# Four small steps after each 192-slot step, joint transposes and alternating block order in a mixture-of-experts stage on one Trainium2 core

## The chip, the cores and the metric

The kernel runs on one core of a Trainium2 chip. The metric is the device time of one execution in microseconds (us), the median of several runs. Engine names: PE is the matrix engine (PEld its weight loads), DVE the vector engine, ACT the scalar engine, POOL the general one, SP the engine whose queue issues the weight transfers.

## The reference, cut to what matters

The reference is a hybrid layer (state space and attention) followed by a second block of two layers, on 256 tokens of width 1024. The change lies wholly in the last stage, the mixture of experts of the second layer:

```
logits = x @ w_router                     # 256 tokens, 8 experts
top_vals, top_idx = top_k(logits, 2)      # two experts for each token
gates = softmax(top_vals)
y = (silu(xb @ w1[e]) * (xb @ w3[e])) @ w2[e]   # for each expert e, on its tokens xb
out = segment_sum(y * gate)               # 1024 -> 3584 -> 1024, in float32
```

After it come a residual sum and a layer norm. Every expert has 3 x 1024 x 3584 float32 weights, 44 MB, so the stage reads 352 MB.

## The kernel before, in words

The experts are ranked by load on the device and renamed: rank 0 has the fewest tokens and so on as the code fixes it. Each rank has a capacity in slots: rank 1 has 192 (a block of 128 slots and one of 64, the latter called number NE = 8), ranks 2 and 3 have 128, ranks 0, 4, 5, 6 and 7 have 64. A block's tokens are gathered into SBUF by one-hot matmuls (`gather`, L1399: matmuls L1416, evictions L1421 and L1423, transposed one-hots L1431, gates L1432).

**A step** is a pair (rank, j): one seventh (512 of 3584 columns) of one expert, NJ = 7 steps for each rank, 56 in all. The list `STEPS` (L218) gives their order. A step reads six weight units of 1 MB, each one transfer into one `raw` buffer: two of w1 and two of w3 (`hidden`, L1510) and two of w2 (`down`, L1571). The matmuls of `down` for step i-1 are placed behind those of `hidden` for step i (`passes`, L1443), and `_moe_order` (L206) gives the units in that order to `rows_unit`, which issues the transfers on SP's queue. From step 2 on six `raw` buffers are in rotation (1 of raw4, 2 of raw2, 3 of rawp; `narrow`, L1306, takes three out), so a transfer waits until the sixth unit before it has been used up.

**Two kinds of block.** A 64-slot block multiplies in plain float32, straight from `raw`, in column pairs (`pair`, L1568: even k into PSUM partitions 0 to 63, odd k into 64 to 127; the two halves are added after a transpose, `turned`, L1550). One such product of one unit shows as 8 PE instructions. A 128-slot block multiplies split operands (`mm3`, L317 to L319, 12 PE instructions a unit); for ranks 1, 2 and 3 (`WIDE`) every unit is therefore split first, in two halves, by a cast on ACT (L298) and a subtraction on DVE (L299).

**After the products of w1 (s) and w3 (t).** For a 64-slot block both are copied to SBUF tiles `eg` by ACT (L1527, three buffers). s is transposed inside `hidden`, behind the first unit of w3 (L1523); t is transposed in `later`, between the two halves of the previous step's `down`. Each transposed product takes a PSUM tile `tp` (two buffers), four PE instructions (L1554) and a reduction on DVE (L1558) that frees it; then silu (L1545) and the product with t (L1546). A 128-slot block multiplies s and t on DVE (L1536), transposes the result (L1539) in one `tp`, and splits it (ACT L354, DVE L355). The first transpose of each group is tied, in PE's order, to the PE instruction traced just before it (`keep_in_program_order`, L1541 and L1556). The rest of each engine's order is fixed by a scheduler when the program is built; on the chip each engine keeps that order.

**PSUM.** Three banks `acc`, three `sm`, two `tp`. A block that is not `aside` accumulates over its seven steps in two `sm` banks. A block that is `aside` (NE, 4, 5, 6 and 7) takes an `acc` and a `sm` bank for each step and adds them into an SBUF tile `y` (DVE L1588; ACT L1586 the first time). When a rank is through, its result is scaled and scattered into the residual (`scaled`, `scatter` L1610).

The order before, as ranks: 0 0 0 4 0 4 0 4 0 4 0 4 4 4, then seven times 1 5 6 7, then seven times 2, then seven times 3. The gathers come in five groups: {4}, {1, NE, 5}, {6, 7}, {2}, {3}; up to step 5 a group is gathered just before its first use, afterwards two steps ahead of it.

Of the kernel before, what the change touches and what calls it, by code (L numbers as in the profile page):

```python
# [8 lines left out]
F32 = mybir.dt.float32  # L9
# [8 lines left out]
P = 128  # L18
D = 1024
# [14 lines left out]
NE = 8  # L34
# [179 lines left out]
    return out  # L214

STEPS = _steps((0, 0, 0, 4, 0, 4, 0, 4, 0, 4, 0, 4, 4, 4) + (1, 5, 6, 7) * NJ + (2,) * NJ + (3,) * NJ)  # L218

WIDE = (1, 2, 3)  # L220

WHOLE = [a + i for a in (0, 52) for i in (1, 2, 3, 4, 15, 16)]

FIXED = [e for e, _ in _moe_order(STEPS)].index(4)

# [14 lines left out]
class Kern:  # L242
# [916 lines left out]
    def moe(self, l, h, hT, out):  # L1159
# [6 lines left out]
        with ExitStack() as ctx:  # L1166
# [142 lines left out]
            def widen():  # L1309
                rctx.close()  # L1310
                more = ctx.enter_context(tc.tile_pool(name="more", bufs=1, side="right"))
                self.xgs = [more] * 4
                self.xns = [more] * 3 + self.xns
                self.ohs = [more] * 4 + self.ohs
                self.ya = more
            es = [nc.sync.value_load(who[0:1, i:i + 1], min_val=0, max_val=NE - 1) for i in range(1, NE)]
# [5 lines left out]
            def rows():  # L1322

                for i in range(2):
                    t = self.ya.tile([P, D], F32, name=f"y{5 + i}")
                    for c in range(2):
                        acc = self.bank([P, 4, P], "acc")
                        for k in range(4):
                            at = KD * i + 4 * c + k
                            mm(acc[:, k], self.gb[:, at:at + 1].to_broadcast([P, P]), self.ident, start=True, stop=True)  # L1330
                        nc.scalar.copy(t[:, 512 * c:512 * c + 512], acc.rearrange("p a b -> p (a b)"))
                    gb.append(t)
                fin.extend(self.ya.tile([P, D], F32, name=n) for n in ("y7", "y8"))
                stats.append(self.mp.tile([P, NT, 2, 6], F32, name="stats"))

            def done(sums):
                self.last_norm(r, sums, fin, stats[0], *gb, out)
            self.passes(posp, gatep, STEPS, r, first, [
                {4: [(4, b)]}, {1: [(1, a), (NE, b)], 5: [(5, b)]},
                {6: [(6, b)], 7: [(7, b)]}, {2: [(2, a)]}, {3: [(3, a)]}], (NE, 4, 5, 6, 7), {2: narrow, 3: widen, len(STEPS) - NJ: rows}, done)  # L1340
            n = nc.values_load(who[0:1, NE + 4:], min_val=0, max_val=4)
            with ExitStack() as some:
                for i in range(4):
# [55 lines left out]
    def gather(self, gate, group, oh):  # L1399

        nc = self.nc
        mm = nc.tensor.matmul
        blocks = sum(group.values(), [])
        starts = [sum(n for _, n in blocks[:i]) for i in range(len(blocks) + 1)]
        width = starts[-1]
        gsl = self.gat.tile([P, 3], F32, name="gsl", bufs=2)
        xs = [tuple(self.turn_of(self.xgs, [P, KD, P], "xg") for _ in range(2)) if n == P else
              (self.turn_of(self.xns, [P, KD, 64], "xn", F32),) for _, n in blocks]  # L1410
        for k in range(0, KD, 2):
            for i, src in enumerate(self.t):
                acc = self.bank([P, 2, 2 * P], "acc")
                for q in range(2):
                    for tb in range(NT):
                        mm(acc[:, q, :width], src[:, tb, (k + q) * P:(k + q + 1) * P], oh[:, tb, :width],  # L1416
                           start=tb == 0, stop=tb == 1)
                for (_, n), at, x in zip(blocks, starts, xs):
                    src, dst = acc[:, :, at:at + n], x[i if n == P else 0][:, k:k + 2]
                    if n == P or i == 0:  # L1420
                        nc.scalar.copy(dst, src)  # L1421
                    else:
                        nc.vector.tensor_add(dst, dst, src)  # L1423
        gp = self.bank([P, 3], "sm")
        out = []
        for i, ((e, n), at, x) in enumerate(zip(blocks, starts, xs)):
            tp = self.bank([P, NT, P], "tp")
            for tb in range(NT):
                o = oh[:, tb, at:at + n].bitcast(F32)
                for a in range(0, P, n):  # L1430
                    mm(tp[a:a + n, tb], o, self.ident, start=True, stop=True)  # L1431
                    mm(gp[a:a + n, i:i + 1], o, gate[:, tb, e:e + 1], start=tb == 0, stop=tb == 1)  # L1432
            ohT = self.turn_of(self.ohs, [P, NT, P], "ohT")
            nc.scalar.copy(ohT, tp)
            out.append((e, x, ohT, gsl[:, i:i + 1]))
        nc.vector.tensor_copy(gsl[:, :len(blocks)], gp[:, :len(blocks)])
        return {e: [out.pop(0) for _ in b] for e, b in group.items()}
# [5 lines left out]
    def passes(self, pos, gate, steps, r, got, groups, aside=(), events={}, done=None):  # L1443

        todo, left, ys = None, None, {}
        groups = list(groups)
        for i, step in enumerate(steps + [None]):
            new = None
            if i in events:
                events[i]()  # L1450

            for e, _ in steps[i:i + (3 if i > 5 else 1)]:
                if e not in got:
                    got.update(self.gather(gate, groups[0], self.one_hot(pos, groups.pop(0))))
            later = None
            if step:
                e, j = step
                out, later = self.hidden([b[1] for b in got[e]])
                new = (e, j, out)
            if left:  # L1460
                self.scatter(left, r)
                left = None
            if not step:
                break
            if todo:
                e, j, gs = todo
                if j == 0:
                    ys[e] = [self.ya.tile([P, D], F32, name=f"y{7 if b[0] == 4 else b[0]}") if b[0] in aside else
                             [self.bank([P, 512], "sm") for _ in range(2)] for b in got[e]]
                    ys[e] = [[y[:, :512], y[:, 512:]] if b[0] in aside else y for y, b in zip(ys[e], got[e])]  # L1470
                here = [b[0] in aside for b in got[e]]
                self.down(ys[e], gs, j, here, (0,))
                later()
                self.down(ys[e], gs, j, here, (1,))
                if j == NJ - 1:
                    left = self.scaled(ys[e], got[e])
            else:
                later()
            todo = new
        done(self.last_sums(r, todo, ys, got, aside))  # L1480
# [29 lines left out]
    def hidden(self, xs):  # L1510


        nc, mp = self.nc, self.mp
        hs = [[], []]
        for i in range(2):
            accs = [self.bank([P, 512], "acc") for _ in xs]
            for k0 in (0, 4):
                w = self.rows_unit(512)
                for x, acc in zip(xs, accs):
                    for k in range(4):  # L1520
                        self.pair(acc, x, k0 + k, w, k, k0 == 0, k0 + 4 == KD, 4)
                if i == 1 and k0 == 0:
                    sums = [self.turned(s, 4) if len(x) == 1 else None for x, s in zip(xs, hs[0])]  # L1523
            for x, acc in zip(xs, accs):
                if len(x) == 1 or i == 0:
                    t = mp.tile([P, 512], F32, name="eg", bufs=3)
                    nc.scalar.activation(t, acc, AF.Copy if len(x) == 1 else AF.Silu)  # L1527
                    acc = t
                hs[i].append(acc)
        out = []  # L1530

        def later():
            for x, s, t, g in zip(xs, *hs, sums):
                if len(x) == 2:
                    gh, gl = (mp.tile([P, 4, P], F32R, name="egs", bufs=4) for _ in range(2))
                    nc.vector.tensor_mul(s, s, t)  # L1536
                    tp = self.bank([P, 4, P], "tp")
                    for k in range(4):
                        t = nc.tensor.transpose(tp[:, k], s[:, k * P:k * P + P], self.ident)  # L1539
                        if k == 0:  # L1540
                            self.tc.keep_in_program_order(t)  # L1541
                    self.split(gh, gl, tp)
                    out.append((gh, gl))
                else:
                    nc.scalar.activation(g, g, AF.Silu)  # L1545
                    nc.vector.tensor_mul(g, g, self.turned(t, 2))  # L1546
                    out.append((g,))
        return out, later

# [21 lines left out]
    def down(self, ys, gs, j, aside, halves=(0, 1), between={}):  # L1571
# [2 lines left out]
                for y, a in zip(ys, aside)]  # L1574
        for c in halves:
            w = self.rows_unit(512)
            for y, g, a in zip(outs, gs, aside):
                for k in range(4):
                    self.pair(y[c], g, k, w, k, a or j == 0, a or j == NJ - 1, 4)
                    if k in between:  # L1580
# [53 lines left out]
```

## Time and profile before

| | |
|---|---|
| median of 3 runs | 2001.63 us (2000.33 to 2001.87) |
| profiled execution | 1999.51 us; its span from first to last instruction 1997.6 us |
| stage of the experts | from about 1010 us of the span to its end |
| busy over the span | PE 95%, PEld 67%, DVE 61%, ACT 44%, POOL 0% |
| transfers of expert weights | 336 of 1 MB, median 7.7 us from issue to landing |

Times of rows are microseconds from the span's start. The busy time of PE is modelled (a matmul's end is reckoned, and successive ones overlap), so the distance between starts says more than the length of one: where starts of the same kind of work lie further apart, PE waited.

### The profile page before, as it was taken

The numbers are of one execution on the slowest core, as the hardware profiler recorded it, in microseconds if no ns is written. First come the engines' busy times: TensorE is split into PE (matmuls) and PEld (weight loads), VectorE is DVE, ScalarE is ACT, GpSimd is POOL, SyncE is SP. The second block draws the span as 40 slices with busy tenths as digits, with TensorE's granted clock in tenths as the row PEclk, the third lists the DMA queues.
The fourth block names the chain that finished last, engine by engine and source line by source line (L and its number), as shares of the span: only waits on it lengthen the run. The fifth ranks groups of instructions, "written<-read, shape, count | busy, mean of one in ns | idle before, by whom it ended". The sixth has DMA issues, their size and how long they took to land.

```text
span 1997.6 us, 27219 instructions
## 1 busy us (share of the span) xinstructions
PE 1903.2 (95%) x10378; PEld 1331.6 (67%) x10378; DVE 1209.3 (61%) x2185; ACT 874.3 (44%) x1411; POOL 8.9 (0%) x21
## 2 busy tenths in 40 slices
PE   7999999998989999998899899999999999999997
PEld 6988888897866999786553245444434444578875
DVE  6547799757896655589731125324433443788887
ACT  4655466344463544355311024323222323567764
POOL 0000000000000000000000000000000000000000
PEclk9999999999998999999899999999999999999998
DMA  5533444454524554563479998988998997998884
GB/s 215 187 138 117 148 153 164 164 200 175 214 97 146 197 194 172 184 215 109 197 279 410 421 421 327 377 346 349 365 383 334 376 373 297 380 347 322 334 329 161
DMA packets 82873, 515.18 MB, mean 258 GB/s; under 512 B 8688, under 2 KB 17568, under 8 KB 22960
## 3 DMA queue, kind: packets, MB, share of 16 engines
q1 hardware_dynamic: 69296, 494.57, 64.5%
q10 hardware_dynamic: 13440, 18.80, 2.9%
q8 instruction: 84, 1.38, 0.3%
q14 instruction: 53, 0.43, 0.1%
HBM read 512.24 MB, written 1.10 MB: 257 GB/s over the span
## 4 chain that ended last, share of the span: by engine, by line
PE 84%; DMA 7%; DVE 6%; ACT 2%; issue 1%; SPq 0%; DVEq 0%; ACTq 0%
PE acc L1568 15%; PE acc L317 14%; PE acc L318 14%; PE acc L319 14%; DMA raw<-in_wm 7%; PE sm L1568 3%; PE acc L329 3%; PE sm L317 2%; PE sm L318 2%; PE sm L319 2%; PE tp L1554 2%; PE acc L351 1%; DVE wlo L299 1%; PE acc L1416 1%; PE acc L1610 1%
## 5 line engine op out<-in xcount | busy, mean ns | idle before, releaser
L299 DVE TENSOR_TENSOR wlo<-raw,whi 128x1024 fp32r<-128x1024 f32 x490 | 583.6, 1221 | 166.5 <-ACT whi L298 165.1
L298 ACT CAST whi<-raw 128x1024 fp32r<-128x1024 f32 x490 | 495.3, 1048 | 188.2 <-PE acc L318 76.4
L1568 PE MATMUL acc<-raw,xn 128*64 128x512 f32 x1344 | 325.2, 599 | 10.0 <-DMA raw<-in_wm 9.8
L1558 DVE TENSOR_REDUCE g<-tp 128x256 f32<-128x512 f32 x84 | 57.9, 690 | 274.8 <-PE tp L1554 274.8
L1568 PEld LDWEIGHTS acc<-raw,xn 128*64 128x64 f32 x1344 | 94.1, 136 | 184.6 <-issue 154.8
L1527 ACT ACTIVATE eg<-acc 128x512 f32<-128x512 f32 x105 | 62.7, 597 | 331.5 <-PE acc L1568 282.2
L317 PE MATMUL acc<-uhi,whi 128*128 128x272 f32 (+1 forms) x576 | 168.8, 293 | 1.4 <-DVE rs_t L375 1.4
L318 PE MATMUL acc<-ulo,whi 128*128 128x272 f32 (+1 forms) x576 | 169.0, 293 | 0.0
L319 PE MATMUL acc<-uhi,wlo 128*128 128x272 f32 (+1 forms) x576 | 167.1, 290 | 0.0
L317 PE MATMUL acc<-hhi,whi 128*128 128x256 f32 x544 | 153.7, 282 | 0.0
L318 PE MATMUL acc<-hlo,whi 128*128 128x256 f32 x544 | 153.2, 282 | 0.0
L319 PE MATMUL acc<-hhi,wlo 128*128 128x256 f32 x544 | 152.6, 281 | 0.0
L317 PE MATMUL acc<-whi,xg 128*128 128x512 f32 x336 | 136.6, 407 | 5.7 <-ACT whi L298 5.7
L318 PE MATMUL acc<-wlo,xg 128*128 128x512 f32 x336 | 136.0, 405 | 1.1 <-DVE wlo L299 1.1
L319 PE MATMUL acc<-whi,xg 128*128 128x512 f32 x336 | 133.4, 397 | 0.0
L317 PEld LDWEIGHTS acc<-uhi,whi 128*128 128x128 f32 x576 | 110.1, 191 | 4.8 <-issue 2.5
L319 PEld LDWEIGHTS acc<-uhi,wlo 128*128 128x128 f32 x576 | 110.0, 191 | 1.8 <-issue 1.5
L318 PEld LDWEIGHTS acc<-ulo,whi 128*128 128x128 f32 x576 | 110.0, 191 | 1.8 <-issue 1.5
L1568 PE MATMUL sm<-raw,g 128*64 128x512 f32 x392 | 103.3, 605 | 1.7 <-DMA raw<-in_wm 1.7
L317 PEld LDWEIGHTS acc<-hhi,whi 128*128 128x128 f32 x544 | 103.2, 190 | 0.2
L318 PEld LDWEIGHTS acc<-hlo,whi 128*128 128x128 f32 x544 | 102.9, 189 | 0.2
L1012 DVE SCALAR_TENSOR_TENSOR cv<-u,cols,cv 128x256 f32<-128x256 f32 x240 | 101.7, 478 | 2.1 <-ACT cv L1010 1.3
(515 smaller groups left out, 3141.9 us busy)
## 6 DMA issues: line engine op xcount, KB each, us to landing
raw<-in_wm SPq DMA_DIRECT2D x336, 1024.0 KB, 7.7
raw<-in_ws SPq DMA_DIRECT2D x131, 1024.0 KB, 4.8
row<-in_rows ACTq DMA_DIRECT2D x9, 512.0 KB, 3.9
seg<-racs ACTq DMA_DIRECT2D x8, 512.0 KB, 3.9
rb<-in_rpb ACTq DMA_DIRECT2D x8, 512.0 KB, 3.4
ck<-rnck ACTq DMA_DIRECT2D x4, 544.0 KB, 3.7
x<-in_x SPq DMA_DIRECT2D x2, 512.0 KB, 5.0
gn<-in_rows ACTq DMA_DIRECT2D x4, 256.0 KB, 3.3
```

Source lines behind the costliest of these rows:

```text
L298: nc.scalar.copy(hi, x)
L299: nc.vector.tensor_sub(lo, x, hi.bitcast(F32))
L317: nc.tensor.matmul(out, lhi, rhi, start=start, stop=False)
L318: nc.tensor.matmul(out, lhi, rlo, start=False, stop=False)
L319: nc.tensor.matmul(out, llo, rhi, start=False, stop=stop)
L329: self.nc.tensor.matmul(out, w.raw[:, k, c:c + P], x[2][:, k, t0:t1], start=k == 0, stop=k == n - 1)
L351: self.nc.tensor.matmul(outs[tb], x[2][:, kk, s], w.raw[:, k], start=start, stop=stop)
L1012: nc.vector.scalar_tensor_tensor(cv[:, m], u[:, m, t:t + T], w, cv[:, m], op0=OP.mult, op1=OP.add)
L1527: nc.scalar.activation(t, acc, AF.Copy if len(x) == 1 else AF.Silu)
L1554: i = self.nc.tensor.transpose(tp[:, k], a[:, k * P:k * P + P], self.ident)
L1558: self.nc.vector.tensor_reduce(g, tp.rearrange("p k (h s) -> p k s h", h=2), axis=AX.X, op=OP.add)
L1568: self.nc.tensor.matmul(out[h:h + 64], x[0][:, kx], w.raw[:, k], start=first and k < 2, stop=last and k >= n - 2)
```

## The change

The order of `STEPS` becomes, as ranks: 0 0 0 0, then seven times one step of rank 1 followed by four small ones taken in the order 0 0 0 4 4 4 4 4 4 4 5 5 5 5 5 5 5 6 6 6 6 6 6 6 7 7 7 7; the remaining three steps of rank 7 stand between those of rank 2 (2 7 2 2 7 2 2 7 2 2), and seven steps of rank 3 end it. The gathers come in four groups, {4, 1, NE}, {5, 6}, {7, 2} and {3}. The 128-slot block of rank 1 becomes `aside`, since its steps now alternate with others that need the banks. s and t of a 64-slot block are both transposed in `later`. In `hidden` and `down` the blocks of a step are taken in turn: 128 then 64 for one unit, 64 then 128 for the next. `gsl` has five buffers instead of two, the tiles `xn` one fewer, and the tiles `y` are shared by other names.

```
-STEPS = _steps((0, 0, 0, 4, 0, 4, 0, 4, 0, 4, 0, 4, 4, 4) + (1, 5, 6, 7) * NJ + (2,) * NJ + (3,) * NJ)
+def _mixed():
+    small = [e for e in (0, 4, 5, 6, 7) for _ in range(NJ)]
+    out = [small.pop(0) for _ in range(4)]
+    for _ in range(NJ):
+        out += [1] + [small.pop(0) for _ in range(4)]
+    for i in range(2 * NJ):
+        out.append(2 if i < NJ else 3)
+        if i % 2 == 0 and small:
+            out.append(small.pop(0))
+    return _steps(out)
+
+STEPS = _mixed()
...
-FIXED = [e for e, _ in _moe_order(STEPS)].index(4)
+FIXED = next(i for i, (e, _) in enumerate(_moe_order(STEPS)) if e)
...
-                self.xns = [more] * 3 + self.xns
+                self.xns = [more] * 2 + self.xns
...
-                fin.extend(self.ya.tile([P, D], F32, name=n) for n in ("y7", "y8"))
...
             def done(sums):
+                if not fin:
+                    fin.extend(self.ya.tile([P, D], F32, name=n) for n in ("y7", "y8"))
                 self.last_norm(r, sums, fin, stats[0], *gb, out)
             self.passes(posp, gatep, STEPS, r, first, [
-                {4: [(4, b)]}, {1: [(1, a), (NE, b)], 5: [(5, b)]},
-                {6: [(6, b)], 7: [(7, b)]}, {2: [(2, a)]}, {3: [(3, a)]}], (NE, 4, 5, 6, 7), ...
+                {4: [(4, b)], 1: [(1, a), (NE, b)]}, {5: [(5, b)], 6: [(6, b)]},
+                {7: [(7, b)], 2: [(2, a)]}, {3: [(3, a)]}], (NE, 1, 4, 5, 6, 7), ...
...
-        gsl = self.gat.tile([P, 3], F32, name="gsl", bufs=2)
+        gsl = self.gat.tile([P, 3], F32, name="gsl", bufs=5)
...
-                    ys[e] = [self.ya.tile([P, D], F32, name=f"y{7 if b[0] == 4 else b[0]}") if b[0] in aside else
+                    ys[e] = [self.ya.tile([P, D], F32, name="y" + ".6..7575"[b[0]] if b[0] < NE else "y8") if b[0] in aside else
...
@@ hidden
-                for x, acc in zip(xs, accs):
+                for x, acc in list(zip(xs, accs))[::1 if k0 == 0 else -1]:
                     for k in range(4):
                         self.pair(acc, x, k0 + k, w, k, k0 == 0, k0 + 4 == KD, 4)
-                if i == 1 and k0 == 0:
-                    sums = [self.turned(s, 4) if len(x) == 1 else None for x, s in zip(xs, hs[0])]
...
-            for x, s, t, g in zip(xs, *hs, sums):
+            for x, s, t in zip(xs, *hs):
...
                 else:
+                    g, t = self.turned(s, 4), self.turned(t, 2)
                     nc.scalar.activation(g, g, AF.Silu)
-                    nc.vector.tensor_mul(g, g, self.turned(t, 2))
+                    nc.vector.tensor_mul(g, g, t)
@@ down
-            for y, g, a in zip(outs, gs, aside):
+            for y, g, a in list(zip(outs, gs, aside))[::1 if c == 0 else -1]:
```

## Rows read from the trace of the kernel before

**Rows 1.** Windows by stage: us, then busy us of each engine, clock, DMA share, GB/s.

```profile
core 0: us, PE busy (x) PEld busy (x) DVE busy (x) ACT busy (x) POOL busy (x), PEclk, DMA share, GB/s
...
1072.50:1166.50 94.00, 80.57 (x375) 25.70 (x371) 14.71 (x24) 10.29 (x20) 0.00 (x0) 1.00 1.01 421
...
1213.70:1731.90 518.20, 512.44 (x2252) 232.44 (x2249) 213.33 (x274) 155.46 (x219) 0.00 (x0) 1.00 0.88 353
1731.90:1981.00 249.10, 246.73 (x1106) 197.81 (x1107) 210.46 (x202) 174.78 (x202) 0.00 (x0) 0.99 0.85 319
```

**Rows 2.** Timeline of PE, a small step at 1084: start, us, instruction [idle before <-releaser].

```profile
1083.82 0.66 PE L1554 MATMUL tp<-cst,eg 128*128 128x128 f32 x4
...
1086.83 1.94 PE L1568 MATMUL acc<-raw,xn 128*64 128x512 f32 x8 [0.49 <-DMA raw<-in_wm]
...
1098.73 0.66 PE L1554 MATMUL tp<-cst,eg 128*128 128x128 f32 x4
```

**Rows 3.** Timeline of PE, the last small step ahead of a 192-slot step.

```profile
1337.56 0.66 PE L1554 MATMUL tp<-cst,eg 128*128 128x128 f32 x4
...
1339.91 5.32 PE L1568 MATMUL acc<-raw,xn 128*64 128x512 f32 x24
1345.16 0.66 PE L1554 MATMUL tp<-cst,eg 128*128 128x128 f32 x4
...
1349.33 0.66 PE L1554 MATMUL tp<-cst,eg 128*128 128x128 f32 x4
1349.92 1.94 PE L1568 MATMUL sm<-raw,g 128*64 128x512 f32 x8
1352.98 0.50 PE L317 MATMUL acc<-whi,xg 128*128 128x512 f32 x1 [1.12 <-ACT whi L298]
```

**Rows 4.** Waits of PE between 1213 and 1729: us in total, times, longest.

```profile
PE acc L317 <- ACT whi L298: 5.3, 5, 1.6
```

**Rows 5.** Timeline of ACT over the same place as rows 3.

```profile
1347.79 0.60 ACT L1527 ACTIVATE eg<-acc 128x512 f32<-128x512 f32 x1 [0.80 <-PE acc L1568]
1351.88 1.99 ACT L298 CAST whi<-raw 128x1024 fp32r<-128x1024 f32 x2 [3.49 <-DMA raw<-in_wm]
```

**Rows 6.** Timeline of PE inside the 192-slot step that follows.

```profile
1362.01 1.94 PE L1568 MATMUL acc<-raw,xn 128*64 128x512 f32 x8
1363.88 0.50 PE L317 MATMUL acc<-whi,xg 128*128 128x512 f32 x1
1364.21 0.39 PE L318 MATMUL acc<-wlo,xg 128*128 128x512 f32 x1
1364.44 0.39 PE L319 MATMUL acc<-whi,xg 128*128 128x512 f32 x1
...
1366.85 1.94 PE L1568 MATMUL acc<-raw,xn 128*64 128x512 f32 x8
...
1375.69 0.66 PE L1539 MATMUL tp<-cst,eg 128*128 128x128 f32 x4
1376.18 0.60 PE L1554 MATMUL tp<-cst,eg 128*128 128x128 f32 x4
1376.71 1.94 PE L1568 MATMUL sm<-raw,g 128*64 128x512 f32 x8
```

**Rows 7.** Timeline of DVE behind those transposes.

```profile
1376.82 0.69 DVE L1558 TENSOR_REDUCE g<-tp 128x256 f32<-128x512 f32 x1 [0.32 <-PE tp L1554]
1377.43 0.68 DVE L355 TENSOR_TENSOR egs<-tp,egs 128x512 fp32r<-128x512 f32 x1
```

**Rows 8.** Timeline of PE, a gather of one block (first and last row).

```profile
1044.53 0.63 PE L1416 MATMUL acc<-oh,thi 128*128 128x64 f32 x4
...
1048.91 1.08 PE L1568 MATMUL acc<-raw,xn 128*64 128x512 f32 x4
```

**Rows 9.** Timeline of PE, the scatter of one 64-slot rank (first row, and the next work).

```profile
1706.09 0.50 PE L1610 MATMUL acc<-yh,ohT 128*128 128x512 f32 x1
...
1708.26 0.64 PE L1568 MATMUL sm<-raw,g 128*64 128x512 f32 x1
```

More of the change, by code (lines that the diff above doesn't have):

```diff
@@ L1332, in rows @@
                     gb.append(t)
-                fin.extend(self.ya.tile([P, D], F32, name=n) for n in ("y7", "y8"))
                 stats.append(self.mp.tile([P, NT, 2, 6], F32, name="stats"))
             def done(sums):
+                if not fin:
+                    fin.extend(self.ya.tile([P, D], F32, name=n) for n in ("y7", "y8"))
                 self.last_norm(r, sums, fin, stats[0], *gb, out)
             self.passes(posp, gatep, STEPS, r, first, [
-                {4: [(4, b)]}, {1: [(1, a), (NE, b)], 5: [(5, b)]},
-                {6: [(6, b)], 7: [(7, b)]}, {2: [(2, a)]}, {3: [(3, a)]}], (NE, 4, 5, 6, 7), {2: narrow, 3: widen, len(STEPS) - NJ: rows}, done)
+                {4: [(4, b)], 1: [(1, a), (NE, b)]}, {5: [(5, b)], 6: [(6, b)]},
+                {7: [(7, b)], 2: [(2, a)]}, {3: [(3, a)]}], (NE, 1, 4, 5, 6, 7), {2: narrow, 3: widen, len(STEPS) - NJ: rows}, done)
             n = nc.values_load(who[0:1, NE + 4:], min_val=0, max_val=4)
```

## The prediction

> **What bounds the kernel now.** I read the windows by stage first, then PE's timeline inside each stage, then what ended PE's waits. The change touches only the stretch from 1010 us on, so the 1010 us before it are taken as unchanged.
>
> The windows [rows 1] show three regimes. From 1072 to 1166, in the list's opening of small steps alone, the transfers run at 421 GB/s, a DMA share of 1.01, while PE is busy 80.6 of 94 us: the transfers bound it. From 1213 to 1731, where each 192-slot step is followed by three small ones, PE is busy 512 of 518 us and the transfers move 353 GB/s. From 1731 to 1981, the 128-slot ranks, PE is busy 247 of 249 us at 319 GB/s. The clock stands at 0.99 to 1.00 in all three, so it is no part of the sum.
>
> A transfer of 1,048,576 bytes at 421 GB/s takes 2.49 us, a step's six 14.9 us. PE's timeline shows both paces of a small step, from one group of transposes to the same group a step later: 1098.73 - 1083.82 = 14.91 us where it waits on `raw` [rows 2], and 1349.33 - 1337.56 = 11.77 us where it doesn't [rows 3]. So the opening loses 3.14 us on each step at the transfers' pace, and 94 / 14.91 = 6.3 such steps lose 19.8 us. That is nearly all the time in the stage that PE could be given back.
>
> The second regime isn't free of it either. PE ends the third small step's work at 1349.92 + 1.94 = 1351.86; the first unit of the next 192-slot step lands just then (ACT begins its cast at 1351.88, released by the transfer [rows 5]), and PE waits 1.12 us for that cast [rows 3]. Five of the seven 192-slot steps have such a wait, 5.3 us together [rows 4]. Three small steps thus use up the whole lead that the transfers gain beside the 192-slot step. Six `raw` buffers hold one step of lead, no more.
>
> **The change part by part**, in us for the whole run, minus is faster.
>
> *The opening goes:* 14 small steps in a row become 4, behind which a 192-slot step stands. The four start with the lead of the first buffers: the stretch at the transfers' pace begins only at 1072 [rows 1]. Minus 19.8.
>
> *A fourth small step in every run:* this gives waits back. A small step after the change (next item) takes PE 11.52 us, its transfers 14.91, and as the lead is used up after three, the fourth costs its whole shortfall, 3.39. The three before it are 0.25 faster each on PE, which the transfers eat as well: 0.75. Seven runs of 4.14 are 29.0 on top of the 5.3 that stay. PE work that needs no weights shortens these waits where it falls inside a run: the gather of {7, 2}, 1048.91 - 1044.53 = 4.4 for one block [rows 8], and the scatters of ranks 4, 5 and 6, each 1708.26 - 1706.09 = 2.2 [rows 9], in all 11.0. Left: plus 18.0. The bounds are 0 (the 192-slot step's slower units refill the lead early enough) and plus 29.
>
> The Trainium skill has a rule for this: Perfetto Trace Analysis, under Identifying Performance Opportunities, Optimization Strategy, says that where the most contended engine changes over time, interleaving the regimes may help. By that rule alone the 19.8 would go and nothing come back. The trace agrees on the two regimes (421 against 319 to 353 GB/s), and speaks against the full gain with the 1.12 us wait at the end of a run of three.
>
> *Both transposes in one place:* a small step's matmuls are now interrupted once instead of twice. Twenty-four matmuls take 1345.16 - 1339.91 = 5.25 [rows 3], so 48 take 10.50; two groups back to back take 1376.71 - 1375.69 = 1.02 [rows 6]; together 11.52 against 11.77. For 35 small steps minus 8.8 (the part that transfers eat is charged above). Bounds: 0, and minus 20 if the second group cost nothing (35 times the 0.58 from 1349.33 to 1349.92). ACT's copy of t, 0.6 [rows 5], is covered as now by the half of `down` in between. The three `eg` buffers suffice: a 192-slot step uses three, all read in `later`, before the next step's first copy. Reductions, silu and product move behind, and have the whole next `hidden` to finish.
>
> *In a 192-slot step three groups stand together* and `tp` has two buffers. The third group waits until DVE's L355 has read the first: 1377.43 + 0.68 = 1378.11 [rows 7], while the second group is through at 1376.71 [rows 6]: 1.4 us. Queued behind on PE is the second half of the previous step's `down`, and the scheduler may put its eight matmuls (1.75) ahead. So 0 to 1.4 for each of 7, 0 to plus 10; I take half, plus 5. These waits fall where the lead is full.
>
> *Alternating block order:* eight 64-column matmuls between wide ones take 1363.88 - 1362.01 = 1.87 instead of 1.75, twelve wide ones 1366.85 - 1363.88 = 2.97 instead of 12 x 0.23 = 2.80 (pitch from 1364.21 to 1364.44) [rows 6]. Two switches cost 0.29, one 0.145. `hidden` goes from 7 switches to 4, `down` gains one inside and loses one at its end: 7 x 0.44, minus 3. Bounds: 0 and minus 6. The three steps of rank 7 between those of rank 2 bring some six new switches: plus 1.
>
> *Costed at nothing:* four groups of gather instead of five, since the one that goes lay in the opening, behind transfers (bounds minus 4.4 to plus 3, as the first group is now three blocks wide and without a step of lookahead). Rank 1's 128-slot block as `aside`: 12 more adds, of about the 0.68 that DVE takes for this shape in L355 [rows 7], 8 us on an engine busy 213 of 518 [rows 1]; were that cover gone, plus 8. In the first 192-slot step rank 0 still holds two `sm` banks and the two blocks share the third: once, about 1. `gsl`, `xn`, the shared `y` and the later `fin` wait for nothing that isn't long done. SP's queue issues the same 336 transfers, in the new order.
>
> Sum: -19.8 + 18.0 - 8.8 + 5 - 3 + 1 = -7.6, say 8. The profiled execution, 1999.51 (span 1997.6 and 1.9 around it), becomes 1991.5; the median of the runs is 2.1 above it, so 1993.5.
>
> **The rivals.**
>
> *Full interleaving.* The runs of four end without new waits. For it: five steps need 30 x 2.49 = 74.6 us of transfers, and PE about 81, namely the second regime's 518.2 / 7 = 74 for four steps with gathers and scatters [rows 1], plus 11.5, less the gains: averaged over a cycle PE is the longer. Against it: the lead is six buffers, and it is empty after three steps now. Then the 18 and half of the third-group wait go: -28, and -40 with the cheap end of the transposes: 1962 to 1974.
>
> *The savings cancel.* Returned waits at 29 rather than 18 give -7.6 + 11 = +3.4; the third group waiting in full gives -7.6 + 5 = -2.6: 1999 to 2005 (both together +8, beyond the case). For it: the terms are of one size, and each rests on a queue that is full or empty by a few us.
>
> *Slower: ACT's order.* ACT keeps the order that was fixed when the program was built. If the cast of a 192-slot step's first unit now stands ahead of the last small step's `eg` copy, PE's transposes, tied to their place, wait for a late transfer, and behind them the half `down` that otherwise fills this time. Behind the landing then come two casts (1.99 [rows 5]), the copy 0.60, both groups 1.02 and eight matmuls 1.75, together 5.4 instead of 1.1: plus 4.3 a cycle. From three of seven cycles (12.9 - 8 = +5) the kernel is slower; all seven give +22, 2024. For it: transfers will be later against PE than now, and the order was reckoned, not measured. Against it: now the copy stands ahead (1347.79 before 1351.88) [rows 5].
>
> **How the numbers follow.** Chances: forecast 0.44 (its own range 1984 to 1999), full interleaving 0.16, cancelled 0.16, slower 0.24. About 4 us, 0.2%, is what a measurement can tell from no change. Faster by more than that: 0.44 + 0.16 less 0.03 of the forecast's upper edge, 0.57; within it 0.16 + 0.03 = 0.19; slower 0.24. The range goes from 1962, the cheap end of full interleaving, to 2014, where four or five cycles of the slower rival stand; some 0.17 is left outside.
>
> **What would show it.** Right: no small step in the opening at 14.9 us between its transposes; DMA share near 1 in each run of four and lower beside the 192-slot step; a wait of 4 to 6 us of PE per cycle, most of it in the fourth small step and ahead of the first wide matmul; small steps of about 11.5 us on PE; a gap of up to 1.4 ahead of the third group of transposes. The forecast is wrong low if runs of four show no wait on `raw`, and wrong high if `eg` copies on ACT stand behind a cast that waits for a transfer, or if PE waits for `acc` or `sm` banks in the 192-slot steps.

## The result, and the profile after

The changed kernel takes 2016.31 us (median of 9 runs), the kernel before 2001.87 beside it: 1.0061 of before, interval 1.0041 to 1.0080. It is slower by 0.6%; 1993.5 was forecast, and 2016 lies 2 above the range. The profiled execution took 2020.28 us (span 2018.5), near the top of its runs, that of before near the bottom of its own, so the two spans differ by 20.9 where the ratio says 12. 1.8 of it lies ahead of the stage.

Windows of the changed kernel, columns as in [rows 1]: the opening with the first 192-slot step, the later cycles (a cycle is a 192-slot step and the four small ones behind it), the ranks 2 with 7 between them:

```profile
core 0: us, PE busy (x) PEld busy (x) DVE busy (x) ACT busy (x) POOL busy (x), PEclk, DMA share, GB/s
1010.00:1100.00 90.00, 87.84 (x453) 40.65 (x452) 25.41 (x51) 25.44 (x51) 0.00 (x0) 1.00 0.83 322
...
1225.10:1682.80 457.70, 439.56 (x2002) 194.59 (x1998) 179.47 (x252) 122.27 (x189) 0.00 (x0) 1.00 0.90 358
1682.80:1866.00 183.20, 170.86 (x737) 115.36 (x736) 116.77 (x119) 94.31 (x115) 0.00 (x0) 0.96 0.94 366
```

The opening isn't at the transfers' pace any more. But PE now idles 18 of 458 us in the cycles (before 6 of 518 [rows 1]) and 12 of 183 behind them, where the clock falls to 0.96 too. PE's waits from 1010 to 1990, before and then after (us in total, times, longest):

```profile
PE acc L1568 <- DMA raw<-in_wm: 11.6, 20, 0.8
PE acc L317 <- ACT whi L298: 5.7, 6, 1.6
PE sm L1568 <- DMA raw<-in_wm: 1.7, 3, 0.6
...
PE acc L318 <- DVE wlo L299: 1.1, 1, 1.1
```

```profile
PE acc L330 <- ACT whi L311: 15.8, 11, 2.0
PE acc L1581 <- DMA raw<-in_wm: 9.2, 18, 0.6
PE acc L331 <- DVE wlo L312: 4.4, 4, 1.5
PE sm L330 <- ACT whi L311: 3.7, 3, 1.6
PE sm L331 <- DVE wlo L312: 1.5, 2, 0.8
...
PE sm L1581 <- DMA raw<-in_wm: 0.6, 1, 0.6
```

Waits for transfers fell from 13.3 to 9.8 us; waits for splits (`whi`, `wlo`) rose from 6.8 to 25.4. They stand in three places. The first is ahead of the first wide matmul behind a run of small steps, that of a 192-slot step or, at 1684, of rank 2: 5.7 before (5.3 of it in [rows 4]), six waits of 1.1 to 2.0, together 8.7, after. In four of the six the cast starts when its weights land, so these 5.35 us are transfers' waits as well:

```profile
1416.33 1.94 PE L1581 MATMUL sm<-raw,g 128*64 128x512 f32 x8
1420.24 0.67 PE L330 MATMUL acc<-whi,xg 128*128 128x512 f32 x1 [1.97 <-ACT whi L311]
```

```profile
1419.14 1.99 ACT L311 CAST whi<-raw 128x1024 fp32r<-128x1024 f32 x2 [1.99 <-DMA raw<-in_wm]
```

In the other two (1.72 and 1.63) the cast starts without idling of ACT, behind a copy of a result of `down`, as it does twice before (at 1282.9, 1.63, and at 1731.9, 0.36). There ACT's order makes PE wait:

```profile
1151.40 0.69 ACT L1611 ACTIVATE yh<-sm,gsl 128x512 fp32r<-128x512 f32 x1 [1.17 <-PE sm L1581]
1151.99 3.99 ACT L311 CAST whi<-raw 128x1024 fp32r<-128x1024 f32 x4
```

The second is new: in `down` of a 192-slot step, behind the `hidden` of the small step that follows. PE, then ACT, of the changed kernel:

```profile
1361.09 6.17 PE L1581 MATMUL acc<-raw,xn 128*64 128x512 f32 x26
1368.94 0.50 PE L330 MATMUL acc<-whi,egs 128*128 128x512 f32 x1 [1.68 <-ACT whi L311]
1369.37 1.93 PE L1581 MATMUL acc<-raw,g 128*64 128x512 f32 x6
```

```profile
1367.36 0.60 ACT L1539 ACTIVATE eg<-acc 128x512 f32<-128x512 f32 x1 [2.89 <-PE acc L1581]
1367.85 3.88 ACT L311 CAST whi<-raw 128x1024 fp32r<-128x1024 f32 x4
```

ACT starts the cast right behind the second `eg` copy, without idling: no transfer is waited for. PE has six plain 64-column matmuls to do, and they stand *behind* the one wide matmul that needs this cast. The same place in the kernel before has the order the other way round, and no wait:

```profile
1316.01 1.88 PE L1568 MATMUL acc<-raw,g 128*64 128x512 f32 x6
1317.82 0.50 PE L317 MATMUL sm<-whi,egs 128*128 128x512 f32 x1
```

ACT's order is the same in both. Four such waits of 1.68 make 6.7 us. The third place is `down` of a rank-2 step behind a rank-7 step's `hidden`: no 64-column product is there to stand in front. PE, then two windows:

```profile
1706.58 3.17 PE L1581 MATMUL acc<-raw,xn 128*64 128x512 f32 x14
1711.38 0.49 PE L330 MATMUL sm<-whi,egs 128*128 128x512 f32 x1 [1.63 <-ACT whi L311]
1712.64 0.50 PE L331 MATMUL sm<-wlo,egs 128*128 128x512 f32 x1 [0.77 <-DVE wlo L312]
...
1714.28 0.63 PE L331 MATMUL sm<-wlo,egs 128*128 128x512 f32 x1
1714.71 0.63 PE L332 MATMUL sm<-whi,egs 128*128 128x512 f32 x1
```

```profile
1711.40:1714.00 2.60, 1.83 (x7) 1.30 (x8) 2.60 (x3) 2.60 (x3) 0.00 (x0) 0.99 1.02 425
1714.00:1717.40 3.40, 3.40 (x12) 2.74 (x11) 1.99 (x2) 2.07 (x3) 0.00 (x0) 0.50 1.01 422
```

All other waits for splits behind the cycles make 10.0 us (1.1 before). And behind the double wait the granted clock is 0.50 for 3.4 us, its lower level of 1.2 GHz: wide matmuls start every 0.43 us instead of 0.23. The changed kernel has six such stretches between 1010 and 1980 (two in the cycles, four among the ranks 2), the kernel before one; each costs 1.7.

The account of the traces: 1.8 ahead of the stage, transfers -3.5, first wide matmuls +3.0, `down` in the cycles +6.7, behind the cycles +8.9, five more half-clock stretches +8.5, in all 25.4; the span grew by 20.9, so PE's own work shrank by some 4.5.

### The profile page after: what moved, and what is told of

Same layout as the page of the kernel before. It is cut to its first block, busy times and chain, and to the rows that moved or that the text cites. A ratio compares the mean times of both kernels' runs of the same rounds, so it can differ in the third digit from the quotient of the medians.

```text
span 2018.5 us, 27137 instructions
## 1 busy us (share of the span) xinstructions
PE 1907.4 (94%) x10346; PEld 1333.7 (66%) x10346; DVE 1215.8 (60%) x2196; ACT 873.8 (43%) x1413; POOL 8.9 (0%) x21
## 4 chain that ended last, share of the span: by engine, by line
PE 84%; DVE 6%; DMA 5%; ACT 3%; issue 1%; SPq 0%; DVEq 0%; ACTq 0%
PE acc L1581 16%; PE acc L330 14%; PE acc L331 14%; PE acc L332 14%; DMA raw<-in_wm 4%; PE sm L1581 4%; PE acc L342 3%; PE sm L330 2%; PE sm L331 2%; PE sm L332 2%; PE tp L1567 2%; ACT whi L311 1%; DVE wlo L312 1%; PE acc L364 1%; PE acc L1430 1%
## 5 line engine op out<-in xcount | busy, mean ns | idle before, releaser
L1581 PE MATMUL acc<-raw,xn 128*64 128x512 f32 x1344 | 319.0, 599 | 6.5 <-DMA raw<-in_wm 6.1
L1601 DVE TENSOR_TENSOR y<-y,acc 128x512 f32<-128x512 f32 x36 | 24.8, 688 | 152.0 <-PE acc L1581 144.3
```

The source lines that it names most:

```text
L1581: self.nc.tensor.matmul(out[h:h + 64], x[0][:, kx], w.raw[:, k], start=first and k < 2, stop=last and k >= n - 2)
L1601: nc.vector.tensor_add(y[c], y[c], o[c])
```

## The experiments

The change has four parts: the **order** of steps, rank 1's 128-slot **block** in `acc` banks (`aside`), the transposes at **one place**, and the **alternation**. Ratios are to the kernel before, which was run beside each; a thousandth is 2 us, and a difference between two of them is sure to some 4 us.

**e1: order and block, without one place and alternation.**

```
-                for x, acc in list(zip(xs, accs))[::1 if k0 == 0 else -1]:
+                for x, acc in zip(xs, accs):
...
+                if i == 1 and k0 == 0:
+                    sums = [self.turned(s, 4) if len(x) == 1 else None for x, s in zip(xs, hs[0])]
...
-                    g, t = self.turned(s, 4), self.turned(t, 2)
...
-            for y, g, a in list(zip(outs, gs, aside))[::1 if c == 0 else -1]:
+            for y, g, a in zip(outs, gs, aside):
```

> The new order of steps (with its fourth small step, its steps among the 128-slot ranks and rank 1's block added up in SBUF) alone; the transposes stay at two places and the block order at 64 before 128. Theory A (the order brings the loss: in the changed kernel ACT casts a wide unit behind the second eg copy of a small step, PE has nothing left to do in front of it, and waits; 28 us of waits on casts against 8.3): no less slow than the changed kernel, since it lacks the joint transposes' and the alternation's gains: 2012 to 2025 where before stands at 2001, with waits on whi and wlo of 20 us or more in the stage and at least three half-clock stretches. Theory B (the transposes at one place bring the loss, through ACT's and PE's changed order and the third group): 1990 to 2003, waits on casts under 12 us. Theory C (the alternation, which makes ACT cast eight in a row, brings it): also 1990 to 2003.

1.0042 (1.0028 to 1.0055), +8.4 us: most of the loss is in the order or the block.

**e2: one place alone**, on the kernel before.

```
-                if i == 1 and k0 == 0:
-                    sums = [self.turned(s, 4) if len(x) == 1 else None for x, s in zip(xs, hs[0])]
...
+                    g, t = self.turned(s, 4), self.turned(t, 2)
```

> The kernel before with both transposes at one place, nothing else. Theory A: -9 to 0 (35 times 0.25 us less the part that transfers eat, plus up to 10 for the third group), so 1993 to 2002 where before stands at 2001. Theory B: +8 to +16, with new waits on whi or egs in most of the seven cycles.

1.0007 (0.9991 to 1.0022): no gain, and no +8 either. PE's waits from 1213 to 1729 show why, against the 5.3 of [rows 4]:

```profile
PE acc L317 <- ACT whi L298: 8.0, 6, 1.9
PE sm L317 <- ACT whi L298: 4.9, 6, 0.8
```

`hidden` without a transpose inside is over sooner, and PE waits for the same cast that it used to meet ready.

**e3: alternation alone**, on the kernel before.

```
-                for x, acc in zip(xs, accs):
+                for x, acc in list(zip(xs, accs))[::1 if k0 == 0 else -1]:
...
-            for y, g, a in zip(outs, gs, aside):
+            for y, g, a in list(zip(outs, gs, aside))[::1 if c == 0 else -1]:
```

> The kernel before with the block order alternating, nothing else. Theory A: -6 to +2 against before. Theory C: +8 to +16, with waits on whi ahead of the first wide matmul of a unit that now begins wide.

0.9950 (0.9935 to 0.9964), -10 us: more than both its bounds.

**e4: the alternation turned about**, in the changed kernel: first the 64-slot block, which needs no cast, then the 128-slot one.

```
-                for x, acc in list(zip(xs, accs))[::1 if k0 == 0 else -1]:
+                for x, acc in list(zip(xs, accs))[::-1 if k0 == 0 else 1]:
...
-            for y, g, a in list(zip(outs, gs, aside))[::1 if c == 0 else -1]:
+            for y, g, a in list(zip(outs, gs, aside))[::-1 if c == 0 else 1]:
```

> The changed kernel with the alternation turned about: in a step of 192 slots the 64-slot block's four matmuls come before the 128-slot block's in the first unit and behind them in the second; the same number of switches between shapes. Theory A (PE waits for casts because a wide matmul now stands first): each of some 15 waits of 1.3 to 2.7 us in the 192-slot steps is shortened by the 0.9 us of four 64-column matmuls, the first by more as they need no cast, and most of the six half-clock stretches (1.7 us each) go: 10 to 22 us faster than the changed kernel, about 1996 to 2006. The rival that the transfers' lead is used up by the fourth small step and the casts come late because the weights do: the wait only moves to the 64-column matmuls (S<-DMA in place of acc<-whi), within 3 us of the changed kernel.

0.9975 (0.9962 to 0.9988), 17 us faster than the changed kernel. The timeline shows `down` behind a small step's `hidden`:

```profile
1355.86 2.30 PE L1581 MATMUL acc<-raw,g 128*64 128x512 f32 x7
1358.12 0.50 PE L330 MATMUL acc<-whi,egs 128*128 128x512 f32 x1
1359.39 0.50 PE L331 MATMUL acc<-wlo,egs 128*128 128x512 f32 x1 [0.76 <-DVE wlo L312]
```

The 1.68 for `whi` is gone, 0.76 for `wlo` is left. Waits for transfers rose from 9.8 to 14.2 (PE from 1010 to 1990), likely since those of the first wide matmuls now show as what they are:

```profile
PE acc L1581 <- DMA raw<-in_wm: 12.9, 25, 0.6
...
PE acc L330 <- ACT whi L311: 1.5, 2, 1.1
```

In the two traces waits for splits fall from 25.4 to 15.5 and the half-clock stretches from six to two (6.8 us). With the transfers' 4.4 more that is 12.3 of the 21.4 by which the spans differ; most of the rest is PE's own time, as in e11.

**e5: the block alone**, on the kernel before.

```
-                self.xns = [more] * 3 + self.xns
+                self.xns = [more] * 2 + self.xns
...
-                {6: [(6, b)], 7: [(7, b)]}, {2: [(2, a)]}, {3: [(3, a)]}], (NE, 4, 5, 6, 7), {2: narrow, 3: widen, len(STEPS) - NJ: rows}, done)
+                {6: [(6, b)], 7: [(7, b)]}, {2: [(2, a)]}, {3: [(3, a)]}], (NE, 1, 4, 5, 6, 7), {2: narrow, 3: widen, len(STEPS) - NJ: rows}, done)
```

> The kernel before with rank 1's 128-slot block of down in acc banks and added up in SBUF, as in the changed kernel (with one gather buffer less to make room); order of steps, transposes and block order as before. Theory D (this block, costed at nothing, is what moves a wide matmul ahead of the 64-column ones behind hidden, in front of a cast that isn't through): in most of the seven cycles PE waits 2.2 us for whi in down where before it waits under 0.7, and half-clock stretches follow some of these: +6 to +14, 2008 to 2016 where before stands at 2002. Rival (the fourth small step is what brings the waits, the block costs nothing): within 3 us of before, no acc<-whi,egs wait over 1 us.

1.0046 (1.0029 to 1.0063), +9.2 us. It has the waits, in the old order of steps, six times 1.63 = 9.8:

```profile
1392.33 0.49 PE L317 MATMUL acc<-whi,egs 128*128 128x512 f32 x1 [1.63 <-ACT whi L298]
1392.76 1.93 PE L1568 MATMUL acc<-raw,g 128*64 128x512 f32 x6
```

So this block alone moves the wide matmul ahead of the plain ones. Beside it the new order neither costs nor gains (e1 less e5: -0.8 us). Its waits brought no half-clock stretch in the cycles of this execution.

**e6: e4 with the transposes at two places** (e1's lines with `turned`, on e4).

> The changed kernel with the 64-slot block first in a step's first unit, and with the two transposes at two places as before: beside the turned-about kernel with the transposes at one place (0.9975 of before) this tells what the one place is worth there. If it saves 0.25 us of each small step and the third group of transposes costs little: 4 to 8 us slower than that kernel, about 2002 to 2006. If the transfers eat the saving in runs of four: within 2 us of it. If the third group costs more than is saved: 2 to 6 us faster.

0.9956 (0.9939 to 0.9973): 3.8 us faster than e4, just within what a difference is sure to. One place costs more than it saves here too, as in the other pairs.

**e7: e4, with rank 7 kept out of the ranks 2.**

```
-    small = [e for e in (0, 4, 5, 6, 7) for _ in range(NJ)]
-    out = [small.pop(0) for _ in range(4)]
+    small = [e for e in (4, 5, 6, 7) for _ in range(NJ)]
+    out = [0] * NJ
...
-    for i in range(2 * NJ):
-        out.append(2 if i < NJ else 3)
-        if i % 2 == 0 and small:
-            out.append(small.pop(0))
+    out += [2] * NJ + [3] * NJ
```

> The turned-about kernel with the three steps of rank 7 taken out from between the steps of rank 2: seven small steps at the opening, then seven times a 192-slot step and four small ones, then the 128-slot ranks alone. In the kernel with them, PE waits some 11 us there for casts (a wide unit of down stands alone behind the small step's hidden), and two to four half-clock stretches fall there. Theory A (these waits go, and the three steps at the opening cost 3 x 3.4 us at the transfers' pace at most, less what the lead covers): 0 to 8 us faster than the turned-about kernel, 1991 to 1999 where before stands at 2002. Rival (the transfers bind there as well, and the waits were slack): 6 to 10 us slower than it.

0.9972 (0.9957 to 0.9987), as e4: inconclusive between the two. In the traces waits for splits fall from 15.5 to 8.3 and those for transfers rise from 14.2 to 18.5: much of what the ranks 2 gain goes where transfers bind.

**e8: one place and alternation**, on the kernel before (the edits of e2 and e3).

> The kernel before with the transposes at one place and the block order alternating (64 before 128 first only in the second unit), its order of steps kept. Alone they gave +1.4 and -10 us. Theory A (the two don't touch each other, all of the loss is the step order's and the block's in acc banks): -12 to -6, 1990 to 1996. Rival (together they put PE in front of the casts): 2000 or more, with waits on whi of over 1.5 us in most cycles.

0.9986 (0.9971 to 1.0001), 2002.56 us: the rival's time, but not its long waits in most cycles; PE's waits for casts are nearly those of e2, from 1010 to 1990:

```profile
PE sm L317 <- ACT whi L298: 4.9, 6, 0.8
```

Beside the alternation one place costs 7 us.

**e9: e6, with the three steps of rank 7 in a row.**

```
-    for i in range(2 * NJ):
-        out.append(2 if i < NJ else 3)
-        if i % 2 == 0 and small:
-            out.append(small.pop(0))
+    out += [2] * 5 + small + [2] * (NJ - 5) + [3] * NJ
```

> The turned-about kernel with the transposes at two places, and the last three steps of rank 7 standing in a row behind the fifth step of rank 2 instead of behind the first, third and fifth. Theory A (a wide unit of down with nothing beside it, behind a small step's hidden, waits 2.2 us for whi and 1.3 for wlo; in a row only the first of the three small steps has such a unit behind it): two such pairs of waits (7 us) and the waits for wlo at the two 128-slot steps behind them go, with up to two half-clock stretches of 1.7 us; the three steps' transfers need 9.4 us more than PE, and the lead is full there: 6 to 12 us faster than the same kernel with them apart (0.9956 of before), 1984 to 1991 where before stands at 2003. Rival (the three in a row wait for transfers what they save on casts): within 3 us of it.

0.9951 (0.9934 to 0.9968), 1 us faster than e6, where 6 to 12 were expected. Of the three waits for a lone wide unit (1.63, 1.63 and 0.64 us) one of 1.63 is left, as expected, and the spans of the profiles are 5.7 apart (1993.2 and 1987.5); over all runs most of that is gone, and where it went stays open.

**e10: e6 with five `raw` buffers.**

```
-            raw2 = ctx.enter_context(tc.tile_pool(name="raw2", bufs=2))
+            raw2 = ctx.enter_context(tc.tile_pool(name="raw2", bufs=1))
...
-            self.raws = [raw2] * 2 + [raw3] * RAW3 + self.raws
+            self.raws = [raw2] * 1 + [raw3] * RAW3 + self.raws
```

> The turned-about kernel with the transposes at two places (0.9956 of before) with one raw buffer less, five instead of six. Theory L (the transfers' lead is what the buffers hold, and it is empty at the end of every run of four): each of the seven runs waits one transfer longer, 2.5 us, most of it on raw: +10 to +17, 2005 to 2012 where before stands at 2003. Rival (the lead isn't used up, the waits for transfers of 15.5 us in its profile are single late ones): within 4 us of it.

1.0052 (1.0036 to 1.0068), 19 us slower than e6. PE's waits from 1010 to 1990, e6 and then e10:

```profile
PE acc L1582 <- DMA raw<-in_wm: 11.3, 21, 0.9
```

```profile
PE acc L1582 <- DMA raw<-in_wm: 22.9, 40, 1.5
```

The lead is what the buffers hold, and runs of four use it up: seven times 2.49 is 17.4, and the waits for transfers rose by 12.2 in the traces.

**e11: the alternation turned about, on the kernel before** (e4's edit on e3).

> The kernel before with the alternation turned about (the 64-slot block first in a step's first unit, last in its second), its order of steps kept. The alternation the other way round gave -10 us there, where -3 was worked out from its switches. If the switches between block shapes are what saves: the same, 1990 to 1997, as both ways have the same number of them. If what saves is which block stands in front of the cast: 3 to 8 us faster still, with the waits for whi ahead of a 192-slot step's first wide matmul gone (six, some 4.5 us).

0.9921 (0.9906 to 0.9936), 1986.77 us: the fastest kernel of the study, 16 us below before, 6 below e3. The expectation for a block in front of the cast has the size right, and the waits for `whi` are gone, but as much for `wlo` came in their place, so waits do not explain the gain; PE's waits from 1213 to 1729, where [rows 4] has 5.3:

```profile
PE sm L318 <- DVE wlo L299: 4.3, 6, 0.7
PE acc L318 <- DVE wlo L299: 1.8, 2, 1.1
...
PE acc L317 <- ACT whi L298: 0.4, 1, 0.4
```

What shrank is PE's own time. The plain (64-column) matmuls alone, from the first wide matmul of the second 192-slot step to that of the seventh, in before, in e12 (e3's program again) and here; the columns are us, PE busy, clock, DMA share, GB/s:

```profile
1282.89:1631.41 348.52, 234.14 (x960) 1.00 0.90 361
```

```profile
1282.96:1626.48 343.52, 229.88 (x960) 1.00 0.92 366
```

```profile
1287.90:1627.10 339.20, 222.37 (x962) 1.00 0.92 372
```

In these five cycles e12 saves 5.0 us, of which 4.3 are the plain matmuls'; e11 saves 9.3, and the plain matmuls are busy 11.8 less. All waits of PE there sum to 4.4, 4.1 and 6.2 us. The traces suggest why. Two plain matmuls that stand next to each other in PE's order mostly start together, 0.01 us apart, and the next two 0.43 later; one whose partner stands elsewhere has such a start to itself. So six take 1.88 us at 1316.01, where eight take 1.94 in [rows 3]. Of the 960, 60 start alone before, 40 in e12 and 20 in e11, which makes 10 and 20 starts less, some 4.3 and 8.6 us. PE also changes between kinds of matmul less often in e11 than in e12 (120 and 144 times), though the loops have the same number of switches. No run varies either alone, so this cause is likely, not shown.

**e12: e3 once more**, one execution.

> The kernel before with the block order alternating, once more: another execution of the same program, whose first profile (2007.97 us, against a median of 1994.41) shows 93.7 us at the granted clock of 0.5 in all. If the difference between executions is this clock: about half of what the half-clock time differs by (a run at 1994 would have some 67 us of it), the span without it within 2 us of 1958.8. Rival (transfers or the start differ): the same half-clock time at another span.

1993.48 us, where e3's own profile had 2007.97. Span and mean granted clock, e3 and then e12:

```profile
core 0: 2005.6 us, clock 0.977
```

```profile
core 0: 1991.6 us, clock 0.986
```

The clock's share lost is 2005.6 x 0.023 = 46 and 1991.6 x 0.014 = 28 us: 18 apart, the spans 14. So the clock is of the size of the difference between two executions of one program, but not all of the account: without its share 1959.5 and 1963.7 us are left, 4 apart where at most 2 was expected.

**e13: order, block and alternation; e14: order, block and one place** (e1 with the edit of e3, and with that of e2).

> The changed kernel with the transposes at two places, its block order alternating as in the change. Its other parts alone gave 1.0042 of before (order and block in acc banks), the alternation alone 0.995. Theory A (with this order and block the alternation, as it stands, saves nothing, as a wide matmul still stands in front of the cast): 2009 to 2015 where before stands at 2003. Rival (the alternation saves its 10 us here too, and all that is lost beside it is the transposes'): 1999 to 2005.

> The changed kernel without the alternation: new order, block in acc banks, transposes at one place. Theory A (one place costs 1 to 7 us, as it did in three pairs of kernels): 2012 to 2020 where before stands at 2003. Rival (the transposes cost some 14 us with this order, and the alternation saves 10): 2022 or more.

1.0037 (1.0027 to 1.0048) and 1.0054 (1.0036 to 1.0072). With this order and block the alternation as changed saves 1 us of its 10, and one place costs 2.4. Both theories A hold.

## Why the prediction was wrong

**The step that failed** is in "Costed at nothing": "Rank 1's 128-slot block as `aside`: 12 more adds, of about the 0.68 that DVE takes ... were that cover gone, plus 8." DVE's adds were indeed covered. What the edit did was to change PE's order: with its results in `acc` banks the wide matmul went in front of the 64-column ones, and PE stood before a cast. That alone is +9.2 us (e5), the shift from -8 to the other side. Why the program's order comes out so, the traces don't show.

A second term failed nearly as far, the transposes at one place. From before by e5, e1 and e13 to the changed kernel one part is added at a time, and the terms stand beside what they measured, each sure to some 4 us: block 0 and +9.2, order of steps -0.8 (its three terms together) and -0.8, alternation -3 and -1.0, one place -3.8 and +4.8.

**The terms, one by one.** Opening -19.8, waits returned +18.0: in the traces, waits for transfers and for the first wide matmul behind a run of small steps are 19.0 before and 18.5 after. In the opening they fall from 13.3 to 0.6; in and behind the cycles they rise from 5.7 to 17.9. The pair was right as a pair, each side of it smaller in waits than forecast, and e10 shows its mechanism, the lead of six buffers. The sign named for it came too. Late in a run of four and then inside the 192-slot step behind it:

```profile
1408.00:1418.00 10.00, 8.43 (x40) 2.97 (x40) 2.31 (x4) 1.55 (x3) 0.00 (x0) 1.00 1.02 420
...
1430.00:1440.00 10.00, 10.00 (x44) 6.01 (x43) 0.00 (x0) 1.69 (x3) 0.00 (x0) 1.00 0.67 246
```

The DMA share sinks from 1.02 to 0.67 beside the 192-slot step, where SP's queue waits for PE to free buffers (up to 7.1 us at a time between 1428 and 1445): the six buffers are full there, and a run of four empties them. The wait per cycle is 0 to 4.0 us, where 4 to 6 was named.

Both transposes together, -8.8, and the third group, +5: the durations were right, the value was not. A small step takes PE 1401.07 - 1389.60 = 11.47 us:

```profile
1389.60 1.09 PE L1567 MATMUL tp<-cst,eg 128*128 128x128 f32 x8
...
1401.07 1.09 PE L1567 MATMUL tp<-cst,eg 128*128 128x128 f32 x8
```

and the third group stands behind two matmuls of `down` that were moved in front of it, as foreseen:

```profile
1356.35 0.60 PE L1567 MATMUL tp<-cst,eg 128*128 128x128 f32 x4
1356.88 1.07 PE L1581 MATMUL sm<-raw,g 128*64 128x512 f32 x2
1357.88 0.66 PE L1567 MATMUL tp<-cst,eg 128*128 128x128 f32 x4
```

But the pair measured +1.4, +7.2, +2.4, +4.8 and +3.8 us (e2, e8 against e3, e14 against e1, the change against e13, e4 against e6) where -3.8 was forecast. Time saved on PE ahead of a wait for a cast or a transfer is given back in that wait (in e2, from 1213 to 1729, 7.6 us more of casts); I had charged that for transfers alone.

Alternation, -3: -10 alone, -4 beside one place (e8 against e2), about 0 beside order and block (e13, and the change against e14). Beside the switches the order of the blocks decides how many plain matmuls start alone (4.3 of 5.0 us in e12, likely) and, in the changed kernel, which block stands in front of a cast (e4). Two readings behind these terms are a little off and move nothing: from 1349.33 to 1349.92 is 0.59, not 0.58, and 12 x 0.23 is 2.76, not 2.80.

The switches of the rank-7 steps, +1, were the wrong thing to count there: behind the cycles, most of it between the ranks 2, stand 8.9 us more of waits for splits and four of the six half-clock stretches, and the clock was to be no part of the sum. With the 64-slot block in front, order and block together cost 7 us (e6 and e11); that the ranks 2 hold it is likely, not shown, as e7 and e9, which take these waits away in two ways, gained little. Beside the block the order costs nothing (e1 and e5); it has three of the waits in `down` where e5 has six, 4.9 us less.

**The rivals.** Full interleaving and cancelling savings fell with the loss. The slower rival named ACT's order, an `eg` copy standing behind a cast that waits for a transfer. That is not what came: the last copy, at 1367.36, stands ahead of the cast at 1367.85. Two of the six waits ahead of a first wide matmul do come from ACT's order, 3.35 us (2.0 before), but behind a copy of a result of `down`. The fixed order that mattered was PE's. The rival's size, up to +22, happened to hold the time; its mechanism is no hit.

## What to carry to other kernels

Where an engine's order is fixed when the program is built, an edit that only moves a result to another bank can reorder that engine; look at the order of the two kernels before costing such an edit at nothing. Ahead of a step that needs a conversion put work that needs none: here turning the order of two blocks about was worth 17 us of 2016, in the two traces somewhat over half of it in waits and clock. The same turn gained 16 us in the old order without less waiting, so look also at how many matmuls that could start together an order tears apart. Time saved in front of a wait counts only as far as the wait does not start sooner.

## What the runs showed of the hardware

The granted clock fell to 0.50 for 3.41 us after PE had stood still in two waits close together (1.63 and 0.77 us at 1711) and at 1420 behind one of 1.97 that followed short waits for transfers. A wait of 1.63 left it at 1.00 in e5's cycles, and so did the same two waits close together (1.63 and 0.76 at 1744) in e4, so the length of these waits does not settle it. The Trainium skill, TensorE: Matmul & The Clock Gate, Part 1, says that activity of the engine releases a clock that is otherwise held at half; that agrees with the lower level of 0.50 seen here, and no run here shows by what it decides. Between two executions of one program its share differed by 18 us where the spans differed by 14 (e3 and e12). Plain matmuls next to each other on PE start 0.01 us apart in twos and 0.43 from one two to the next at a granted clock of 1.00: six of them, two without a partner, took 1.88 us and eight 1.94.
